# In-projection of a hybrid encoder layer: casts of the weights placed behind the copy that empties the product's bank, on ScalarE, in all blocks of tokens

## The chip, the cores and the metric

One core of a Trainium2 chip runs the whole kernel. The metric is the device time of one execution in microseconds (us). Before the change the median of three runs is 2311.37 us (2309.41 to 2311.43). The profile is of a further execution of its own, which took 2306.19 us.

## What is computed

The reference is one layer of a streaming encoder, applied to a prompt of 2048 tokens and to a batch of 8 sample sequences of 16 tokens each. Cut to what matters here:

```python
qm, km, vm, om, ip, fp, qa, ka, va = split_in(x @ w_in)        # the in-projection, D_MODEL = 1024
km = km * (M_HEAD_DIM ** -0.5)
hm, C1, n1, m1 = mlstm_chunkwise(qm, km, vm, logi, logf, C0, n0, m0, mchunk)   # 4 heads of 128
hm = (sigmoid(om) * head_norm(hm, g_mlstm_norm))
qa, ka = rope(qa, pos), rope(ka, pos)
ha = swa_prompt(qa, ka, va, attn_sinks)                        # window attention, 8 heads of 64
mix = concatenate([hm, ha], axis=-1) @ w_out                   # the out-projection
h = layer_norm(DEEPNORM_ALPHA * x + mix, ln1_g, ln1_b)
f, conv_rows = conv_ffn(h, conv_prev, w_up, w_conv, b_conv, w_down)
y = layer_norm(DEEPNORM_ALPHA * h + f, ln2_g, ln2_b)
```

The first line is the stage that the change touches. Its result is split into q and k of the mLSTM (a matrix memory with gates), its values v, its output gate, two small gates, and q, k and v of the window attention.

## The kernel before, in words

**Stages.** The kernel goes through the in-projection (about the first 620 us), the out-projection, the up-projection with its convolution (L1874) and the down-projection (L2084). TensorE does all the matrix products. Each operand in float32 is first split into a high half and a low half in a reduced format, and three products replace one (high by high, high by low, low by high). The split of one unit of weights is two instructions in `split`: a cast on ScalarE (L218) from the raw weights `wraw` to the high half, and a subtraction on VectorE (L219) that leaves the low half. VectorE's part needs the result of ScalarE's.

**The in-projection.** `i_dense` (L588) walks over four blocks `b` of four token tiles each (128 tokens a tile; block 0 has the sample tile besides). In each block it walks over five groups `g` of output columns: 0 and 1 are q and k of the mLSTM, 2 is q of the attention (which then gets its rotation, `rope`), 3 is the output gate (which goes through a tanh) and 4 is v. Two by two blocks of a product are computed with seven products instead of eight, by sums of operands (the method of Strassen and Winograd); the products are numbered `s` and come in the order 1, 7, 6, 2, 5, 3, 4 or one close to it. Each product is `i_product` (L693): 24 matmuls of 128x128 by 128x256 (L705) into one of three banks of PSUM, A, B and C, which are called `dps` in the profile. Products 1 and 2 go to A, products 6, 5 and 3 to B, 7 and 4 to C. Between the products stand "direct" items, one for each token tile, for the small gates and the keys and values of the attention.

**What empties a bank.** Behind each product `i_after` (L769) is traced, at high priority. Depending on `s` it does this:

- s = 1, only at g = 0: ScalarE copies A to B (L780), so that the following products add to the sum there.
- s = 6: ScalarE copies B to a buffer (`zev` in the profile) through the small function `copy` of L772, which scales by a constant for g < 2.
- s = 2: `i_out` (L756) copies A to a buffer on ScalarE (L764, or the tanh of L761 for g = 3) and stores it to DRAM.
- s = 5: ScalarE copies B (L772), VectorE adds C to the copy, and `i_out` stores the sum.
- s = 4: VectorE adds C to the buffer of s = 6, and `i_out` stores it. ScalarE has no copy here.
- s = 3: `i_out` copies B to a buffer (L764 or L761) and stores it, and then ScalarE copies A to B for the next group (L800).

**Weights.** Behind `i_after`, `i_dense` calls `advance` (L415). It splits as many of the next units of weights as there is room for: the ring of split weights holds four units of two halves (`w` in the profile), and each product that ends frees one unit. It also issues the loads of further raw weights on SyncE's queue, into seven slots; some units are sums that are kept in DRAM and are loaded as they are. So the cast of L218 is released by the last matmul of the product that freed its place, which is also what releases the copies of `i_after`.

**Work woven in.** The class `Chains` weaves other work into the blocks, tile by tile, as the inputs of it are there: the mLSTM tiles (`m_tile`, with the matmuls `pnum` of L1212), their norm (`m_norm`: `mr` on VectorE in L1154 to L1160, `ms` on GpSimd in L1161, the scaling `hn` on ScalarE in L1167, the transpositions `pht` of L1177 on TensorE), the window attention (`swa`: scores L1304, exponentials on ScalarE L1316, their division on ScalarE L1321, the transpositions `ppt` of L1343 on TensorE, the products `ppo` of L1349), and the sample tile's attention (L1518). VectorE also takes the sums of weights for the next stages (`txy`, L851 to L857) and the rotations (`rope`).

**Order.** TensorE's order is written out by hand: the order in which the program traces its matmuls is the order in its queue. The other engines' queues are ordered by a scheduler, which weighs priorities and its own estimate of when each instruction is ready. `tc.issue_after(ins)` is a context for that scheduler: whatever is traced inside and goes to the queue of an engine that `ins` uses is put behind `ins` in that queue. It adds no wait on a result, only an order. Before the change it was used at one place and for one kind of product:

```python
680            with self.tc.issue_after(behind) if behind and b == 0 else nullcontext():
681                self.advance()
```

`behind` is what `i_after` returned, and that was an instruction only for s = 1 at g = 0 (L780), `None` otherwise.

Of the kernel before, what the change touches and what calls it, by code (L numbers as in the profile page):

```python
# [10 lines left out]
AF = mybir.ActivationFunctionType  # L11
# [18 lines left out]
KSCALE = float(np.float32(128.0 ** -0.5))  # L30
# [175 lines left out]
class Prog:  # L206
# [381 lines left out]
    def i_dense(self):  # L588
        nc, a = self.nc, self.a
        nb = len(IBLOCKS)  # L590
        last = NG - 1

        self.next_raw()
        self.x_load(0, 2)
        for _ in range(3):
            self.next_raw()
        self.x_load(0, 4)
        self.single_raw = self.tp.tile([P, KD, P], F32, name="xsr", tag="pth", bufs=2)
        nc.sync.dma_start(self.single_raw, a["xs"])
        self.angles = {}  # L600
        self.rope_load(IBLOCKS[0][2], 2)
        self.rope_load(NPT, 1)
        self.next_split()
        self.x_steps(0, "b12")
        for _ in range(3):
            self.next_split()
        self.x_steps(0, 3)
        self.x_single(1, 2)
        self.x_load(0, 1)
        self.next_raw()  # L610
        self.x_load(0, 3)
        self.x_steps(0, 1)
        self.advance()
        self.x_steps(0, 2, "t3", 7, "t2", 6)
        self.x_single(4)
        self.x_steps(0, "t1", 5, "t4")
        self.sb, self.trans = {}, None

        passages = [{1: ["load"], 7: ["t3", 7], 6: ["t2", 6], 3: [3, "t4"], 4: ["b12", "t1"]},
                    {1: ["load"], 6: ["t3"], 7: [7, "t2"], 5: [6], 3: [3, "t4"], 4: ["b12", "t1"]}]  # L620
        sums = 0
        after = None
        for item in self.items:
            if after:

                after[0] -= 1
                if after[0] == 3:
                    self.logs_of(after[1] - 1)
                if after[0] < 0:
                    self.i_done = after[1]  # L630
                    after = None
            self.chains.hold = item[0] == "t" and item[1] > 0
            if item[0] == "t":
                _, b, ti, e = item
                if ("g", e, 3) not in self.wu:
                    self.advance()
                if b not in self.gates:
                    self.gates[b] = self.tp.tile([P, 5, 8], F32, name="gates", tag="gates", bufs=2)
                ps = self.bank([P, 512], "pg") if ti == 4 else self.ib[ti % 2 * 2]
                yield from self.i_direct(b, ti, e, ps)  # L640
                self.i_keys(b, ti, ps)
                if ti == 1:
                    if b + 1 < nb:
                        self.x_steps(b + 1, 1, 2)
                    else:
                        self.release(4)
                    after = [6, b + 1]
                elif ti == 3 and b or ti == 4:
                    self.release(4)
                    self.x_steps(b, 4)  # L650
                    if b:
                        self.x_steps(b, 5)
                self.advance()
                continue
            _, b, g, s = item
            if item not in self.wu:
                self.advance()
            yield from self.i_product(b, g, s)
            del self.wu[item]
            self.release(2)  # L660
            if self.trans and s != 4:
                self.i_transposes()
            with self.tc.high_priority():
                behind = self.i_after(b, g, s)
            if (b, g, s) == (0, 0, 7):
                self.t_setup()
            if (g, s) == (1, 6):
                self.rope_load(IBLOCKS[b][0], 2)
            if g == last and b + 1 < nb:
                if s == 7:  # L670
                    self.rope_load(IBLOCKS[b + 1][2], 2)
                for x in passages[b > 0].get(s, ()):
                    if x == "load":
                        self.spare = True
                        self.x_load(b + 1, 1, 2, 3, 4)
                    else:
                        self.x_steps(b + 1, x)
            if g == last and b + 1 == nb and s in (7, 5, 2, 3):
                self.x_pair(0, (7, 5, 2, 3).index(s))
            with self.tc.issue_after(behind) if behind and b == 0 else nullcontext():  # L680
                self.advance()

            if b >= nb // 2 and g < last:

                steps = (6, 2, 5) if g == last - 1 else (6, 5, 3)
                if s in steps:
                    self.d_sums(sums, steps.index(s))
                    sums += s == steps[2]
        self.sums = sums
        self.logs_of(nb - 1)  # L690
        self.chains.hold = False
# [64 lines left out]
    def i_out(self, b, g, i, j, src):  # L756

        nc = self.nc
        ev = src if i else self.zev()
        if g == 3:  # L760
            nc.scalar.activation(ev, src, AF.Tanh, scale=0.5)  # L761
            nc.vector.tensor_scalar_add(ev, ev, 1.0)
        elif not i:
            nc.scalar.copy(ev, src)  # L764
        if g == 2:
            self.rope(ev, IBLOCKS[b][2 * j], 2)
        self.i_store(b, g, i, j, ev)

    def i_after(self, b, g, s):  # L769
        nc, V = self.nc, self.nc.vector  # L770
        A, B, C = self.ib
        copy = lambda d, x: nc.scalar.activation(d, x, AF.Copy, scale=KSCALE) if g < 2 else nc.scalar.copy(d, x)  # L772

        def add(u):
            if g < 2:
                V.scalar_tensor_tensor(u, C, KSCALE, u, op0=ALU.mult, op1=ALU.add)
            else:
                V.tensor_add(u, C, u)
        if s == 1 and g == 0:
            return nc.scalar.copy(B, A).ins  # L780
        elif s == 6:
            self.u2 = self.zev()
            copy(self.u2, B)
        elif s == 2:
            self.i_out(b, g, 0, 0, A)
        elif s == 5:
            u4 = self.zev()
            copy(u4, B)
            add(u4)
            self.i_out(b, g, 1, 1, u4)  # L790
        elif s == 4:
            add(self.u2)
            self.i_out(b, g, 1, 0, self.u2)
            if b == 0:
                self.i_batch(g)
        elif s == 3:
            self.i_out(b, g, 0, 1, B)
            if g + 1 < NG:

                nc.scalar.copy(B, A)  # L800

    def i_batch(self, g):

# [1383 lines left out]
```

## Time and profile before

| | us |
|---|---|
| median of three runs | 2311.37 |
| lowest and highest of them | 2309.41, 2311.43 |
| profiled execution | 2306.19 |
| its span in the profile | 2304.4 |
| mean granted clock of TensorE | 0.997 |
| TensorE busy in the span | 2279.1 |

The span goes from the first to the last recorded instruction of the profiled execution; the execution's time is 1.8 us longer than it. Times in rows of a timeline are us from the span's start, then the duration; a name in brackets tells for how long the engine was idle before and what ended that. In the rows of groups, waits and timelines, the names stand as output<-inputs, and L is the line of the kernel before. PE is TensorE's matmuls, PEld its loads of weights, DVE is VectorE, ACT is ScalarE, POOL is GpSimd and SP is SyncE. "Granted clock" is the share of full speed that the chip let TensorE have, 1.00 being all of it.

### The profile page before, as it was taken

Reading aid. Unit: us, or ns where it says so; the run is one execution under the profiler, and the core shown is the slowest. Engines: PE = TensorE matmul, PEld = TensorE weight load, DVE = VectorE, ACT = ScalarE, POOL = GpSimd, SP = SyncE. Lnnn points to the kernel's source line nnn. Section 1 sums busy time; section 2 is a strip of 40 time slices with the busy share of each in tenths; the row PEclk is TensorE's granted clock in tenths of the full one; section 3 lists DMA queues with packets and bytes.
Section 4 is the critical chain, followed back from the end, with each engine's and each line's share of the span. In section 5 each row is a group of like instructions: output and inputs, shape, how many; then the busy total and the mean of one; then the engine's idle time right before and its main releaser. Section 6 shows DMA issues by size and latency. Waiting matters only on the chain.

```text
span 2304.4 us, 39746 instructions
## 1 busy us (share of the span) xinstructions
PE 2279.1 (99%) x14293; PEld 2093.5 (91%) x14293; DVE 1807.5 (78%) x3075; ACT 1272.6 (55%) x2377; POOL 272.7 (12%) x509
## 2 busy tenths in 40 slices
PE   8999999999999999999999999999999999999998
PEld 8999999999877778999999999999999988888876
DVE  8787587787688878998778777678766786895987
ACT  4453476776766656555656555555555544444442
POOL 0001001000011210211112100003111200100100
PEclk9999999999999999999999999999999999999999
DMA  7988999999987757888778889978998786756742
GB/s 265 320 303 298 311 321 342 312 305 345 313 285 241 239 196 278 306 320 307 277 276 279 302 307 308 320 263 290 318 293 262 230 294 214 256 167 222 254 154 84
DMA packets 300165, 632.38 MB, mean 274 GB/s; under 512 B 47868, under 2 KB 141120, under 8 KB 299968
## 3 DMA queue, kind: packets, MB, share of 16 engines
q1 hardware_dynamic: 295296, 616.14, 77.8%
q0 software_dynamic: 3520, 10.56, 1.4%
q10 hardware_dynamic: 1152, 3.15, 0.4%
q8 instruction: 113, 1.85, 0.3%
q14 instruction: 84, 0.69, 0.1%
HBM read 458.11 MB, written 171.64 MB: 273 GB/s over the span
## 4 chain that ended last, share of the span: by engine, by line
PE 81%; DVE 4%; DMA 1%; issue 1%; ACT 1%; POOL 0%; SPq 0%; DVEq 0%; ACTq 0%; POOLq 0%
PE dps L1874 19%; PE fup L1874 19%; PE dps L705 7%; PE fup L2084 7%; PE dps L2084 6%; PE fht L2084 6%; PE dps L223 3%; PE dps L224 2%; PE dps L225 2%; PE ppo L1349 1%; PE psc L1304 1%; PE ppt L1343 1%; PE dps L731 1%; PE fht L1698 1%; DVE w L219 1%
## 5 line engine op out<-in xcount | busy, mean ns | idle before, releaser
L1874 PE MATMUL dps<-hh,uw 128*128 128x384 f32 (+1 forms) x1848 | 478.0, 328 | 2.1 <-DVE u L1905 2.1
L1874 PE MATMUL fup<-hh,uw 128*128 128x384 f32 (+1 forms) x1848 | 478.0, 328 | 0.0
L1874 PEld LDWEIGHTS dps<-hh,uw 128*128 128x128 f32 x1848 | 330.0, 188 | 2.4 <-DVE u L1905 2.4
L1874 PEld LDWEIGHTS fup<-hh,uw 128*128 128x128 f32 x1848 | 330.0, 188 | 0.0
L1931 DVE SCALAR_TENSOR_TENSOR cc<-u,cw,cc 128x768 f32<-128x768 f32 (+1 forms) x264 | 257.9, 977 | 63.7 <-ACT cc L1929 56.9
L1874 PE MATMUL fup<-hl,uw 128*128 128x384 f32 (+1 forms) x924 | 302.7, 328 | 0.9 <-DVE hl L219 0.9
L1874 PE MATMUL dps<-hl,uw 128*128 128x384 f32 (+1 forms) x924 | 302.3, 327 | 0.0
L705 PE MATMUL dps<-w,oh 128*128 128x256 f32 x1344 | 254.2, 284 | 0.0
L218 ACT CAST uw<-wraw 128x1024 fp32r<-128x1024 f32 x126 | 123.2, 978 | 231.4 <-PE dps L2084 122.4
L219 DVE TENSOR_TENSOR w<-wraw,w 128x1024 fp32r<-128x1024 f32 (+2 forms) x167 | 189.3, 1140 | 67.0 <-ACT w L218 64.6
L218 ACT CAST w<-wraw 128x1024 fp32r<-128x1024 f32 (+2 forms) x167 | 163.0, 984 | 121.3 <-PE dps L705 63.4
L705 PEld LDWEIGHTS dps<-w,oh 128*128 128x128 f32 x1344 | 210.4, 188 | 10.9 <-issue 8.1
L219 DVE TENSOR_TENSOR uw<-wraw,uw 128x1024 fp32r<-128x1024 f32 x126 | 142.4, 1130 | 65.7 <-ACT uw L218 64.0
L705 PE MATMUL dps<-w,ol 128*128 128x256 f32 x672 | 187.8, 279 | 0.0
L1874 PEld LDWEIGHTS fup<-hl,uw 128*128 128x128 f32 x924 | 173.5, 188 | 1.6 <-DVE hl L219 1.5
L2084 PE MATMUL fup<-uw,fu 128*128 128x512 f32 x726 | 173.7, 396 | 0.0
L1874 PEld LDWEIGHTS dps<-hl,uw 128*128 128x128 f32 x924 | 173.5, 188 | 0.0
L705 PE MATMUL dps<-oh,w 128*128 128x256 f32 x896 | 169.7, 284 | 3.6 <-DVE w L219 1.3
L2084 PE MATMUL dps<-uw,fu 128*128 128x512 f32 x660 | 165.3, 396 | 1.1 <-DVE uw L219 1.1
L2084 PEld LDWEIGHTS fup<-uw,fu 128*128 128x128 f32 x726 | 136.3, 188 | 33.1
L1929 ACT ACTIVATE cc<-u,cw 128x768 f32<-128x768 f32 (+1 forms) x132 | 132.2, 1001 | 49.2 <-DVE u L1911 23.9
L2084 PEld LDWEIGHTS dps<-uw,fu 128*128 128x128 f32 x660 | 123.8, 188 | 31.5 <-DVE uw L219 1.5
(318 smaller groups left out, 4577.9 us busy)
## 6 DMA issues: line engine op xcount, KB each, us to landing
uw<-zw SPq DMA_DIRECT2D x176, 512.0 KB, 5.0
zw<-uw SPq DMA_DIRECT2D x88, 512.0 KB, 3.5
w<-zws SPq DMA_DIRECT2D x72, 512.0 KB, 5.9
wv<-wup SPq DMA_DIRECT2D x66, 512.0 KB, 4.6
wraw<-wi SPq DMA_DIRECT2D x65, 512.0 KB, 6.1
wraw<-zt SPq DMA_DIRECT2D x60, 512.0 KB, 3.9
wraw<-wdn SPq DMA_DIRECT2D x45, 512.0 KB, 4.5
wraw<-wo SPq DMA_DIRECT2D x40, 512.0 KB, 4.7
```

Of the source, the lines that this page charges most:

```text
L218: nc.scalar.copy(hi, src)
L219: nc.vector.tensor_sub(lo, src, hi.bitcast(F32))
L223: mm(out, ah, bh, start=start, stop=False)
L224: mm(out, ah, bl, start=False, stop=False)
L225: mm(out, al, bh, start=False, stop=stop)
L705: mm(o, l, r, start=s in (1, 7) and c == k == i == 0, stop=k == 3 and i == 2, skip_group_check=True)
L731: mm(o, x, w, start=k == i == 0, stop=k == KD - 1 and i == 2, skip_group_check=True)
L1304: nc.tensor.matmul(ps[kvh][:, j, :nk], q[rs, j0 + j], k[rs, sel], start=i == 0, stop=i == 2)
L1874: mm(ps, l[:, k], r[:, k], start=s in (1, 7) and k == 0 and i == 0, stop=k == 3 and i == 2, skip_group_check=True)
L1929: S.activation(c[:, v], u[:, 2:2 + n], AF.Identity, bias=w[3], scale=w[2])
L1931: V.scalar_tensor_tensor(c[:, v], u[:, i:i + n], w[i], c[:, v], op0=ALU.mult, op1=ALU.add)
L2084: mm(ps, l[:, k, c], r[:, k], start=s in (1, 4, 7) and u == 0 and k == 0 and i == 0, stop=u == nu - 1 and k == n - 1 and i == 2, skip_grou ...
```

## The change

Two things are edited. The condition `b == 0` goes, so that the ordering context is entered in each block. And `i_after` now returns, for s = 6, 2, 5 and 3 also, the ScalarE instruction that empties the bank; `i_out` returns it to `i_after`. For s = 3 with a further group to come it is the copy from A to B that is returned (the last of the two). For s = 4, and for s = 1 at g > 0, there is still nothing to return, and the call of `advance` stands as before. No instruction is added or taken away.

```diff
@@ i_dense
-            with self.tc.issue_after(behind) if behind and b == 0 else nullcontext():
+            with self.tc.issue_after(behind) if behind else nullcontext():
                 self.advance()
@@ i_out
         ev = src if i else self.zev()
+        emptied = None
         if g == 3:
-            nc.scalar.activation(ev, src, AF.Tanh, scale=0.5)
+            emptied = nc.scalar.activation(ev, src, AF.Tanh, scale=0.5).ins
             nc.vector.tensor_scalar_add(ev, ev, 1.0)
         elif not i:
-            nc.scalar.copy(ev, src)
+            emptied = nc.scalar.copy(ev, src).ins
...
         self.i_store(b, g, i, j, ev)
+        return emptied
@@ i_after
-        copy = lambda d, x: nc.scalar.activation(d, x, AF.Copy, scale=KSCALE) if g < 2 else nc.scalar.copy(d, x)
+        copy = lambda d, x: (nc.scalar.activation(d, x, AF.Copy, scale=KSCALE) if g < 2 else nc.scalar.copy(d, x)).ins
...
         elif s == 6:
             self.u2 = self.zev()
-            copy(self.u2, B)
+            return copy(self.u2, B)
         elif s == 2:
-            self.i_out(b, g, 0, 0, A)
+            return self.i_out(b, g, 0, 0, A)
         elif s == 5:
             u4 = self.zev()
-            copy(u4, B)
+            emptied = copy(u4, B)
             add(u4)
             self.i_out(b, g, 1, 1, u4)
+            return emptied
...
         elif s == 3:
-            self.i_out(b, g, 0, 1, B)
+            emptied = self.i_out(b, g, 0, 1, B)
             if g + 1 < NG:
 
-                nc.scalar.copy(B, A)
+                emptied = nc.scalar.copy(B, A).ins
+            return emptied
```

## The prediction

> **What bounds the kernel now.** I read the totals first, then the waits of the matrix engine, then single stretches. Line numbers are those of the profile of before.
>
> ```profile
> PE 2279.1 (99%) x14293; PEld 2093.5 (91%) x14293; DVE 1807.5 (78%) x3075; ACT 1272.6 (55%) x2377; POOL 272.7 (12%) x509
> ```
> ```profile
> 0.00:46.00 46.00, 38.59 (x238) 35.12 (x239) 39.32 (x66) 24.78 (x40) 0.31 (x5) 0.89 0.73 260
> 46.00:620.00 574.00, 567.93 (x4867) 538.53 (x4868) 421.42 (x971) 347.90 (x775) 46.32 (x70) 1.00 0.93 317
> 100.00:200.00 100.00, 100.00 (x868) 99.47 (x867) 81.00 (x131) 53.05 (x76) 1.92 (x3) 1.00 0.87 304
> ```
>
> TensorE bounds it. The second fence is the table of stretches (length, then busy time of PE, weight load, VectorE, ScalarE, GpSimd, then granted clock). The in-projection, the only stage that the change touches, ends near 620 us. After its first 46 us TensorE stands still for 574.00 - 567.93 = 6.1 us in all: no reordering of ScalarE there can gain more than about that. Instructions start 100/868 us = 0.115 us apart, so a product of 24 matmuls takes 2.8 us.
>
> ```profile
> PE ppt L1518 <- POOL v L1094: 2.9, 1, 2.9
> PE dps L705 <- DVE w L219: 1.3, 2, 0.8
> PE pht L1177 <- DVE ql L219: 1.1, 1, 1.1
> PE dps L705 <- ACT mr L1154: 0.9, 1, 0.9
> PE pnum L1212 <- issue: 0.5, 1, 0.5
> ```
>
> These are the waits of TensorE (total us, times, longest). They are single events: one in the sample attention (2.9), two for weights (both before 41 us), one behind ql, one that the profile puts down to mr, one at pnum. There is no steady wait for a bank to be emptied.
>
> **What the change does in the queues.** As built, the order of TensorE and GpSimd stays as it is, instruction for instruction. ScalarE, VectorE and the SP queue are reordered up to the end of the in-projection and no further. Nothing is added or removed. In ScalarE's queue 47 of the 167 casts of weights now stand behind copies of a product's bank that they stood ahead of. The usual place before:
>
> ```profile
> 57.63 1.05 ACT L218 CAST w<-wraw 128x1024 fp32r<-128x1024 f32 x1 [1.26 <-PE dps L705]
> 58.58 0.58 ACT L834 COPY zev<-pxt 128x512 f32<-128x512 f32 x1
> 59.06 0.59 ACT L764 COPY zev<-dps 128x512 f32<-128x512 f32 x1
> 59.69 0.57 ACT L800 COPY dps<-dps 128x512 f32<-128x512 f32 x1
> ```
>
> Cast and copies are released by the end of the same product; the cast went first, so the copies came 0.95 us later (58.58 - 57.63). Now they go first and the cast starts up to 1.7 us later.
>
> *Copies earlier.* A bank is written again after at least one other product (2.8 us), and cast plus copies took 2.6 us (57.63 to 60.26), so the copy was mostly in time and moving it is worth nothing. Once it was not:
>
> ```profile
> 327.01 1.04 ACT L218 CAST w<-wraw 128x1024 fp32r<-128x1024 f32 x1
> 327.95 0.59 ACT L772 ACTIVATE zev<-dps 128x512 f32<-128x512 f32 x1
> 327.37 0.28 PE L705 MATMUL dps<-oh,w 128*128 128x256 f32 x1
> 328.60 0.38 PE L705 MATMUL dps<-oh,w 128*128 128x256 f32 x1 [0.95 <-ACT mr L1154]
> ```
>
> The matmul after 327.37 waits until the copy ends (327.95 + 0.59), whatever the name in brackets. In the new order the copy stands ahead of that cast and of four divisions. The gap goes: 1.23 between starts less 0.115 is 1.1 us.
>
> *Casts later.* They feed products that lie three or more ahead (some 8 us), and since 41 us TensorE waited for no weight. 1.7 us of delay and the VectorE half behind it (1.22 us) stay inside that: zero. The SP queue's loads of raw weights wait for the cast and go 1 or 2 us later, with the same cover; without it each late unit would cost up to 1.7 us.
>
> *VectorE's side effects.* In the first tile of block 1 the low half of a weight (L219) now stands behind the step that pnum waits for:
>
> ```profile
> 318.86 1.21 DVE L219 TENSOR_TENSOR w<-wraw,w 128x1024 fp32r<-128x1024 f32 x1
> 319.99 0.68 DVE L1133 TENSOR_TENSOR dt<-pscore,dt 128x512 f32<-128x512 f32 x1
> 320.77 0.46 PE L1212 MATMUL pnum<-v,dt 128*128 128x129 f32 x2 [0.48 <-issue]
> ```
>
> pnum starts 0.1 us after L1133 ends. L1133 would come 1.13 us earlier, but one 0.7 us step of L854 slips in ahead: most of the 0.5 us gap goes. In block 2 the order puts L853 behind the low half of q:
>
> ```profile
> 514.26 0.69 DVE L853 TENSOR_TENSOR txy<-txy 128x512 f32<-128x512 f32 x1
> 514.87 0.68 DVE L219 TENSOR_TENSOR ql<-pq,qh 128x512 fp32r<-128x512 f32 x1
> 515.61 0.66 PE L1177 MATMUL pht<-ident,hn 128*128 128x128 f32 x4 [1.14 <-DVE ql L219]
> ```
>
> ql gains 514.87 - 514.26 = 0.6 us, and so does pht. In the sample attention (the 2.9 us) VectorE's work ahead of the exponentials is only shuffled; I put it at 0, bounds -0.7 and +0.7 (one step of a rotary or of L853, as the row of L853 has it).
>
> *The loss.* In that same first tile the eighth division of the attention (L1321), the last one, now stands behind four scalings hn (L1167) and the copy L764, while the other three of its group stand ahead of them, behind two casts. Before, all were done early:
>
> ```profile
> 325.25 1.86 ACT L1321 ACTIVATE sc<-sc,asm 128x128 f32<-128x128 f32 x6
> 332.23 1.04 PE L1343 MATMUL ppt<-ident,sc 128*128 128x128 f32 x8
> 332.26 0.15 DVE L1160 TENSOR_TENSOR mr<-mr,bmv 128x4 f32<-128x4 f32 x1
> 332.56 1.37 POOL L1161 TENSOR_TENSOR ms<-mr,mhalf 128x4 f32<-128x4 f32 x1 [9.60 <-DVE mr L1160]
> 333.96 0.69 ACT L1167 ACTIVATE hn<-hn,ms 128x128 f32<-128x128 f32 x2 [2.89 <-POOL ms L1161]
> 334.56 0.57 ACT L764 COPY zev<-dps 128x512 f32<-128x512 f32 x1
> 335.07 0.74 PE L1177 MATMUL pht<-ident,hn 128*128 128x128 f32 x3
> 336.30 0.33 PE L1177 MATMUL pht<-ident,hn 128*128 128x128 f32 x1 [0.48 <-ACT hn L1167]
> ```
>
> hn waits for GpSimd's ms, which waits for VectorE's mr; TensorE's eighth transposition (332.23 + 7 x 0.11 = 333.0) needs that division. Behind the waiting hn are the copy, the division and TensorE. The new times: mr loses one L219 ahead of it (-1.2) and gains a reciprocal (+0.2), so 331.3; ms 331.6 to 332.9; four hn at 0.30 to 0.35 until 334.2; copy until 334.7; division (1.86/6 = 0.3) until 335.0. The transposition moves from 333.0 to 335.0, and TensorE, which comes there 1.1 + 0.5 us sooner, stands 2.0 + 1.6 = 3.6 us. The hn then no longer hold pht (335.07 + 3 x 0.11 = 335.4 against 336.30: 0.9 saved). Net from 318 to 337, the gains there included: +2.0 - 0.9 = +1.1. If VectorE brings mr no earlier, everything is 1.0 later: +2.1. Neither excludes the other; I take +1.5.
>
> A long hold costs more than itself, as the start shows:
>
> ```profile
> 39.45 0.39 PE L705 MATMUL dps<-oh,w 128*128 128x256 f32 x1 [0.68 <-ACT w L218]
> 40.79 0.39 PE L705 MATMUL dps<-oh,w 128*128 128x256 f32 x1 [0.84 <-DVE w L219]
> 40.00:42.00 2.00, 1.21 (x7) 1.21 (x8) 2.00 (x3) 2.00 (x3) 0.00 (x0) 0.83 0.96 379
> 42.00:44.00 2.00, 2.00 (x12) 2.00 (x11) 2.00 (x4) 0.24 (x1) 0.00 (x0) 0.50 0.58 174
> 44.00:46.00 2.00, 1.31 (x8) 1.11 (x8) 1.97 (x3) 0.79 (x2) 0.00 (x0) 0.82 0.83 215
> 250.00:255.00 5.00, 2.15 (x21) 1.87 (x19) 1.00 (x4) 1.70 (x8) 1.19 (x2) 1.00 0.95 315
> ```
>
> After two gaps of 0.7 and 0.8 us the granted clock is short by (0.17 + 0.50 + 0.18) x 2 = 1.7 us. The 2.9 us of the sample attention left it at 1.00. A hold of 3.6 us is longer than both; I count the 1.7 (bounds 0 and 1.7). [...]
>
> The sum: +1.5 + 1.7 - 0.6 = +2.6 us. The profiled execution took 2306.19 us, its span 2304.4; so 2308.8 for it. The median of the runs shown, 2311.37, lies 5.2 above that execution, hence **2314.0 us**.
>
> **The rivals.** *Only the gains (A).* If ms is early enough, nothing is held at ppt, and 1.1 + 0.5 + 0.9 + 0.6 = 3.1 us go: 2308.3. For it: copies do go first. Against: hn waited 2.89 us for GpSimd where it stands now. Its limit is 6.1 us, 2305.3.
>
> *Casts behind waiting copies delay VectorE (B), slower.* VectorE runs its queue in order too, and its low halves wait for casts already:
>
> ```profile
> DVE w L219 <- ACT w L218: 60.2, 49, 4.9
> ```
>
> With the cast 0.6 us later (one copy), what stands behind an L219 on VectorE (mr, dt, ql) is 0.6 us later; it counts where TensorE has less margin than that, as ql at 515.61 has none. [...] Eight tiles are woven into the blocks; from all eight on it is 8 x 0.6 = 4.8 us more: 2318.8. Against: VectorE is idle a quarter of the stretch (421.42 of 574).
>
> *The change does nothing (C).* If the copies were never late and the division is in time after all: 2311.4. The one copy at 327.95 speaks against.
>
> **How the numbers follow.** Forecast 0.47, A 0.17, B 0.28, C 0.08. 0.2% is 4.6 us, about what a measurement of this kernel can tell from no change. Faster by more needs A near its limit: 0.08. Slower by more than 4.6 (above 2316.0) is B, plus 0.05 for a forecast whose hold is longer than worked out: 0.33. The rest, 0.59, is within. The range goes from A's limit, 2305, to B with its own upper bounds: 2318.8 + 1.7 (a second stretch at half clock) + 0.6 (2.1 in place of 1.5) + 0.7 = 2322. The forecast alone, with 0.9 and 2.1 + 1.7 + 0.7, spans 2312 to 2316.
>
> **What would show it.** A new wait of TensorE at ppt L1343 of 3 to 4 us near 331, with hn and a copy just ahead of the division on ScalarE, and a granted clock under 1.00 in the microseconds after it: right. The gaps at pnum (320.8) and before 328.6 gone: right. No such wait at ppt: A. Many new waits of 0.3 to 1 us at pht, pnum and ppo: B. TensorE waiting for weights (L219) after 46 us would make the zero for the casts wrong, and a shift after 620 us the claim that only this stage moves.

## The result, and the profile after

Over 20 runs each the changed kernel takes 2311.47 us (2310.06 to 2315.33) and the kernel before 2308.07 us (2303.73 to 2311.43). The ratio is 1.0015, with a 95% interval of 1.0010 to 1.0021: the change costs 3.4 us (2.3 to 4.8). A second set, shared with experiments, gives 1.0019 (1.0010 to 1.0028). Two of the three runs from which the prediction started are the longest of the twenty, so its 2314.0 is 2.5 us high, though the change it forecast is 0.8 us too small.

The profiled execution after took 2315.33 us, 9.1 above the profiled one before; both lie towards the ends of their twenty. So the traces are read for places, and the sum is taken from the medians. The lines up to `i_out` keep their numbers; from there on 1 to 4 are added (L764 is now L765, L1343 is L1347), and in an experiment a few more or fewer, by its edit.

The stretch of the in-projection, from the table of stretches (the prediction shows the same row of before: PE busy 567.93, clock 1.00), and then TensorE's waits in it:

```profile
46.00:620.00 574.00, 562.62 (x4808) 534.43 (x4807) 415.22 (x962) 339.55 (x755) 47.63 (x68) 0.99 0.91 312
```
```profile
PE ppt L1347 <- ACT sc L1325: 4.4, 2, 3.9
...
PE ppt L1347 <- ACT pth L1348: 1.4, 1, 1.4
PE dps L705 <- DMA w<-zws: 1.2, 1, 1.2
PE dps L705 <- ACT dps L803: 0.9, 1, 0.9
PE ppt L1347 <- DVE C L1228: 0.7, 1, 0.7
```

TensorE now stands still for 574.00 - 562.62 = 11.4 us, against 6.1. The waits at pnum, at pht and for the copy near 328 us are no longer in the list; new on top is ppt, behind a division (L1325), which is the hold. In time order, from the timeline of after:

```profile
329.22 0.99 ACT L1325 ACTIVATE sc<-sc,asm 128x128 f32<-128x128 f32 x3 [1.12 <-DVE asm L1323]
329.68 0.95 PE L1347 MATMUL ppt<-ident,sc 128*128 128x128 f32 x5 [0.48 <-ACT sc L1325]
329.93 2.50 POOL L1165 TENSOR_TENSOR ms<-mr,mhalf 128x4 f32<-128x4 f32 x1 [9.15 <-ACT sc L1325]
332.46 1.28 ACT L1171 ACTIVATE hn<-hn,ms 128x128 f32<-128x128 f32 x4 [2.25 <-POOL ms L1165]
333.64 0.56 ACT L765 COPY zev<-dps 128x512 f32<-128x512 f32 x1
334.11 0.40 ACT L1325 ACTIVATE sc<-sc,asm 128x128 f32<-128x128 f32 x1
334.56 0.47 PE L1347 MATMUL ppt<-ident,sc 128*128 128x128 f32 x1 [3.94 <-ACT sc L1325]
```

ScalarE runs three divisions, then waits 2.25 us for GpSimd with hn at the head of its queue; the four hn, a copy and only then the eighth division follow, and TensorE's eighth transposition has waited 3.94 us for it. What that does to the clock, from the table of stretches (granted clock behind the five busy times):

```profile
332.00:334.00 2.00, 0.00 (x0) 0.00 (x0) 1.62 (x3) 1.54 (x5) 1.01 (x2) 0.75 1.06 409
334.00:336.00 2.00, 1.44 (x7) 1.44 (x8) 0.00 (x1) 2.00 (x5) 0.19 (x1) 0.50 0.84 328
336.00:338.00 2.00, 2.00 (x11) 2.00 (x11) 1.78 (x2) 2.00 (x6) 0.00 (x0) 0.50 0.56 185
338.00:340.00 2.00, 2.00 (x12) 2.00 (x11) 0.33 (x2) 0.62 (x3) 0.00 (x0) 0.55 1.01 335
```

The clock is short by (0.25 + 0.50 + 0.50 + 0.45) x 2 = 3.4 us, that is half clock for 6.8 us; of these TensorE had work in the last 5.2 (1.44 + 2.00 + 1.80). At half clock the matmuls of a product start 0.21 us apart (336.33 to 336.97 for three) in place of 0.115, so it lost about 2.5 us there. What the whole place costs is read from two matmuls that stand on either side of it, in before and in after:

```profile
320.01 0.28 PE L705 MATMUL dps<-oh,w 128*128 128x256 f32 x1
339.01 1.08 PE L1349 MATMUL ppo<-pth,kva 128*64 128x512 f32 x4
```
```profile
318.30 0.28 PE L705 MATMUL dps<-oh,w 128*128 128x256 f32 x1
342.11 1.08 PE L1353 MATMUL ppo<-pth,kva 128*64 128x512 f32 x4
```

Before, 19.00 us lie between them, after 23.81: the place costs 4.8 us net, gains and clock included.

Behind it there is more. In the last block (b = 3) VectorE stands at the first step of a sum (txy), which waits for its load; the rows are of after and of before:

```profile
544.85 0.69 DVE L855 TENSOR_TENSOR txy<-txy 128x512 f32<-128x512 f32 x1 [7.47 <-DMA txy<-wdn]
```
```profile
536.28 0.69 DVE L851 TENSOR_TENSOR txy<-txy 128x512 f32<-128x512 f32 x1 [3.71 <-DMA txy<-wdn]
```

Behind that step stand VectorE's update of C (the wait of 0.7 at ppt in the list) and mr, on which hn waits, and behind hn the copies pth (the 1.4). The load is late on the queue of SP, here of before and then of after:

```profile
524.67 0.42 SPq L857 DMA_DIRECT2D zt<-txy  x1
528.52 0.37 SPq L750 DMA_DIRECT2D zqk<-zev  x1
528.94 0.54 SPq L845 DMA_DIRECT2D txy<-wdn  x1
```
```profile
533.52 0.37 SPq L750 DMA_DIRECT2D zqk<-zev  x1
533.95 0.62 SPq L861 DMA_DIRECT2D zt<-txy  x1
538.99 0.33 SPq L849 DMA_DIRECT2D txy<-wdn  x1
```

The store of the last sum (zt) used to be ahead of the store of a product (L750), which waits for ScalarE's copy; now it is behind it, and the next load, which needs the same buffer, waits for that store to land: SP's queue stands 4.3 us at it.

### The profile page after: what moved, and what is told of

Read it like the earlier page. It is cut to its first block, busy times and chain, and to the rows that moved or that the text cites. A ratio compares the mean times of both kernels' runs of the same rounds, so it can differ in the third digit from the quotient of the medians.

```text
span 2313.6 us, 39735 instructions
## 1 busy us (share of the span) xinstructions
PE 2282.5 (99%) x14293; PEld 2097.3 (91%) x14293; DVE 1807.5 (78%) x3075; ACT 1272.1 (55%) x2377; POOL 282.7 (12%) x509
## 4 chain that ended last, share of the span: by engine, by line
PE 81%; DVE 4%; DMA 1%; issue 1%; ACT 1%; SPq 0%; POOL 0%; DVEq 0%; ACTq 0%; POOLq 0%
PE dps L1878 19%; PE fup L1878 19%; PE dps L705 8%; PE fup L2088 7%; PE dps L2088 6%; PE fht L2088 6%; PE dps L223 3%; PE dps L224 2%; PE dps L225 2%; PE ppo L1353 1%; PE ppt L1347 1%; PE psc L1308 1%; PE dps L731 1%; PE fht L1702 1%; DMA txy<-wdn 1%
## 5 line engine op out<-in xcount | busy, mean ns | idle before, releaser
L219 DVE TENSOR_TENSOR w<-wraw,w 128x1024 fp32r<-128x1024 f32 (+2 forms) x167 | 189.1, 1142 | 59.4 <-ACT w L218 54.8
L219 DVE TENSOR_TENSOR uw<-wraw,uw 128x1024 fp32r<-128x1024 f32 x126 | 142.7, 1132 | 64.3 <-ACT uw L218 64.0
```

What stands on the lines that cost most here:

```text
L219: nc.vector.tensor_sub(lo, src, hi.bitcast(F32))
```

## The experiments

Theory H: the change costs what the hold of TensorE at ppt and the clock behind it cost. Rival B: casts behind copies make VectorE, the loads and with them much else late. T (the loads of the sums) and L (TensorE runs so close to its loads that time won is given back) came up on the way. All ratios are to the kernel before, run on the same chip. The sets a1 and e1 to e3, e4 to e7, e8 and e9, and e10 and e11 ran on four chips, so medians are compared within a set and ratios across.

| run | median, us | ratio (95%) |
|---|---|---|
| a1, the change again | 2313.46 | 1.0019 (1.0010 to 1.0028) |
| e1, one product taken out | 2309.82 | 1.0003 (0.9994 to 1.0012) |
| e2, last block only | 2308.33 | 0.9998 (0.9989 to 1.0007) |
| e3, all but the last block | 2315.67 | 1.0030 (1.0021 to 1.0039) |
| e4, the change, division first | 2311.36 | 1.0011 (1.0002 to 1.0020) |
| e5, third block only | 2311.03 | 1.0005 (0.9996 to 1.0014) |
| e6, before again | 2309.54 (one run) | |
| e7, as e3, again | 2318.82 (one run) | |
| e8, before, sums later | 2311.39 | 1.0021 (1.0010 to 1.0033) |
| e9, the change, sums later | 2319.09 | 1.0053 (1.0039 to 1.0066) |
| e10, before with a hold alone | 2317.55 | 1.0032 (1.0020 to 1.0044) |
| e11, as e4, one sum later | 2313.96 | 1.0023 (1.0013 to 1.0033) |

**The change again.** No edit.

> The changed kernel as it is, a second profile of it. Theory H (the eighth division of the first attention tile stands behind hn on ScalarE and holds TensorE at ppt, and the hold spoils the clock): about 2311.5 us, a wait at ppt near 330 us of 3.5 to 4.5 us, a granted clock under 1.00 just behind it; the other new gaps of the first profile (1.1 us near 370, 1.4 near 393, 2.4 near 546 to 553) are accidents of that execution and are mostly gone. Theory B (casts behind copies make VectorE, SP's loads and with them much else late): the same time, but these other gaps come again at the same places, 4.9 us in all.

TensorE's waits in this execution:

```profile
PE ppt L1347 <- ACT sc L1325: 4.4, 2, 3.9
...
PE dps L705 <- DMA w<-zws: 0.8, 1, 0.8
...
PE ppt L1347 <- ACT pth L1348: 0.6, 1, 0.6
```

The hold comes again to the tenth. Of the other new waits, the 0.9 for the copy L803 and the 0.7 behind C are gone, and those for w and behind pth are there at 0.8 and 0.6. The wait for w is not the same one, though: it stands at 393.7 us in the first profile and at 579.6 in this one. Of the 4.9 us that B wanted at the same places, only the 0.6 behind pth comes again, so here H is nearer. Still, both profiles wait for w somewhere, and neither profile of before does behind 46 us.

**The hold taken away, by one product.**

```diff
-            with self.tc.issue_after(behind) if behind else nullcontext():
+            with self.tc.issue_after(behind) if behind and (b, g, s) != (2, 0, 5) else nullcontext():
```

> The change with one product (b = 2, g = 0, s = 5) taken out of it; as built this puts the eighth division ahead of hn again, and moves few other instructions. H: the hold of about 4 us and the clock loss of 1.5 us go, the 1.0 us gap before the product behind it and 0.7 us at pht come back: 2311.5 - 3.8 = 2307.7 us, equal to before. B: 54 of 55 places are as in the change: 2310.5 to 2312 us.

```profile
PE pht L1181 <- ACT hn L1171: 2.0, 3, 1.1
```

No hold, 2.0 us at pht in its place, and 3.6 us less than the change on the same chip (2313.46 - 2309.82), where H said 3.8. With one product taken out, nothing clear of noise is left of the loss. The same two matmuls on either side of the place, in e1:

```profile
319.61 0.28 PE L705 MATMUL dps<-oh,w 128*128 128x256 f32 x1
338.89 1.08 PE L1353 MATMUL ppo<-pth,kva 128*64 128x512 f32 x4
```

They lie 19.3 us apart: 0.3 more than before, where the change had 4.8 more (5.0 in a1).

**The hold alone, in the kernel before.** In `swa`, for t = 0, the last of the eight divisions is not issued with the others:

```diff
-            self.nc.scalar.activation(hn[:, h], hn[:, h], AF.Copy, scale=s[:, h:h + 1])
+            self.scaled = self.nc.scalar.activation(hn[:, h], hn[:, h], AF.Copy, scale=s[:, h:h + 1]).ins
...
+                if t == 0 and j == 3 and len(z) == 2 and sc is z[1][0]:
+                    self.last_division = lambda: nc.scalar.activation(sc[:, 3, :N], sc[:, 3, :N], AF.Copy, scale=sm[:, 3:4])
+                    continue
...
+                    if t == 0 and (kt, kvh, j) == (0, 1, 3):
+                        with self.tc.issue_after(self.scaled):
+                            self.last_division()
                     nc.tensor.transpose(pp[:, j * P:(j + 1) * P], scs[j // 2][...], self.ident)
```

> The kernel before with the last division of the first attention tile alone moved on ScalarE: behind hn, and with it behind two copies, a cast and the first copy of ppt; nothing of the change is in it. The division comes near 338.0 us (the last hn ends at 336.2, then 1.05 + 0.56 + 0.3), TensorE wants it at 333.0: a hold of 5.0 us, less 0.9 at pht behind it, and 1.7 us of clock. H (a hold of TensorE costs its length to the end): 2308.7 + 5.8 = 2314.5 us. Theory L (TensorE runs so close to its loads that a hold is partly given back in shorter waits later): 2310 to 2312 us. B: 2308.7 us.

The waits of TensorE:

```profile
PE ppt L1349 <- ACT sc L1322: 5.2, 1, 5.2
...
PE pht L1177 <- DVE ql L219: 2.5, 1, 2.5
```
The two matmuls around the place:

```profile
319.54 0.28 PE L705 MATMUL dps<-oh,w 128*128 128x256 f32 x1
344.28 1.08 PE L1355 MATMUL ppo<-pth,kva 128*64 128x512 f32 x4
```

A hold of 5.2 us, with nothing else of the change, costs 7.4 us by the ratio (4.6 to 10.2), which bears H out; nothing is given back here, against L. The place itself costs 5.7 us (24.7 against 19.0), where H said 5.8. What goes beyond lies elsewhere and is not shown to come from the hold: the wait at ql grew from 1.1 us (before) to 2.5, and one of 1.8 us is new near 1650 us, far behind the in-projection (see the end).

Counted in this way, the place separates the runs: it takes 23.6 to 24.0 us in the four profiles of the change's hold (after, a1, e3, e7), 19.0 and 19.1 in the two of before, and 19.0 to 19.8 in the five of the change, or of parts of it, without the hold and with the sums where they were (e1, e2, e4, e5, e11).

**By blocks.**

```diff
-            with self.tc.issue_after(behind) if behind else nullcontext():
+            with self.tc.issue_after(behind) if behind and (b == 3 or (b, g, s) == (0, 0, 1)) else nullcontext():
```

For the run of all but the last block the condition is `b != 3`, for that of the third block `b == 2`, each with the same exception.

> The change in the last block (b = 3) alone. H: no hold, only the gain at ql near 515 us (1.1 us): 2307.0 us, at or just under before. B: the load of txy that waits for the store of the sums, and with it VectorE's work and ppt near 546 to 553 us, is late by itself: + 2.4 - 1.1 = 2309.5 us.

> The change in the blocks b = 0, 1 and 2, as before in the last. H: the whole loss is there, and the gain at ql is not: 2312 us. B: the loss of the last block (1.3 us net) is gone: 2310 us.

> The change in the block b = 2 alone, the one into which the first attention tile is woven; as built all eight divisions stand ahead of hn. H: gains without the hold: 0.7 (pnum) + 1.1 (before 328.6) + 0.5 (pht): 2308.6 - 2.3 = 2306.3 us. B: a third of the loss: 2310 us.

The last block alone costs nothing (0.9998): its wait at ql is gone, and in exchange VectorE waits longer for its sum and 1.1 us are lost at ppt. So B's mechanism for the last block is there in this profile and just pays for the gain; the second profile of before (below) shows how much of such waits is chance:

```profile
537.24 0.69 DVE L855 TENSOR_TENSOR txy<-txy 128x512 f32<-128x512 f32 x1 [6.38 <-DMA txy<-wdn]
```

All but the last block holds TensorE as the change does and keeps the old order in the last one; by H it should have cost what the change costs, and it cost 7 us (0.0030 x 2308.87). The third block alone should have won 2.3 us, since it has the gains and not the hold. It won nothing (1.0005): here the expectation missed. Two of its waits:

```profile
PE ppo L1353 <- ACT pth L1348: 1.8, 1, 1.8
PE pht L1181 <- DVE ql L219: 1.7, 1, 1.7
```

pnum and the gap near 328 us are gone, but at the place itself the wait for hn has grown from 0.5 to 1.1 us and two of 0.5 us for copies are new, so it takes 19.8 us in place of 19.0; behind it a wait at ppo is new and the one at ql has grown. The parts don't add up: -0.5 for the last block and +7 for the others make more than the 3.4 to 4.4 of the whole. In e3 the place costs no more than in the change (23.6 us); 1.5 us of its 7 are a wait near 1645 us that no profile of the change has, and the gain at ql is missing.

**Second looks.** e6 is the kernel before and e7 the kernel of e3, each with another profile.

> The kernel before, a second profile of it, to tell what is its own from what an execution adds by chance. H and B alike: waits at pnum, before 328.6, at pht near 335 and at pht near 515 us again; nothing over 0.3 us at ppt or ppo between 330 and 345; VectorE's wait for the load of txy near 535 us under 4.5 us. Single stretches of 3.4 us at half clock may come or go.

> The change in the blocks b = 0, 1 and 2 once more; nine executions of it took 2311 to 2319 us while the one with a profile took 2311.5. H: if this execution is one of 2315 or more, it has a further stretch of 3.4 us at a granted clock of about 0.5 behind a wait of TensorE, 1.7 us for each, and no more waits than the first. B: it has waits of 1 us or more after 340 us that the first has not, for weights, txy or copies.

The kernel before waits at the expected places, but ppo shows 1.8 us where the first profile showed none, and VectorE waited 5.32 us for the sum's load near 537 us (3.71 in the first). So waits behind such loads of 1 to 2 us are in part chance. In e7 TensorE waits 5.5 us in such places, and it was 2318.82. Of these, 3.2 us lie in the last block; the 2.3 at ppt come at 660.9 us, behind the in-projection, and there the clock is short by 1.7 us as well (0.89 over 655 to 670 us; 1.00 in e3). So both sides of that expectation came: new waits, which B had and H had not, and a further stretch at half clock, as H said.

```profile
PE ppt L1347 <- ACT pth L1348: 2.3, 1, 2.3
PE ppo L1353 <- ACT pth L1348: 1.6, 1, 1.6
PE pht L1181 <- DVE ql L219: 1.6, 1, 1.6
```

**The hold taken away by priority.**

```diff
-        divided(*z[1])
+        with self.tc.high_priority() if t == 0 else nullcontext():
+            divided(*z[1])
```

> The whole change, with the last four divisions of the first attention tile alone at high priority, so that none of them stands behind hn on ScalarE; the copy still goes ahead of its casts there. H: no hold of 3.9 us at ppt near 330 and no clock loss behind it, and the gap before 328 us stays gone too; against the change (2312.2 us over both sets of runs) - 3.9 - 1.5 + 0.5 (hn holds pht for a moment instead) = 2307.3 us, 1 to 2 us under before. B: 2311 to 2313 us, as the change.

The hold is gone, but only about two microseconds were won, within the noise (1.0011 against 1.0019). The gap near 328 us did not stay gone: at 326.33 TensorE waits 0.79 us for the copy, which now stands behind the four divisions. The first fence has rows of the timeline (VectorE, ScalarE, TensorE, and then SP's queue), the second two rows of the table of stretches:

```profile
352.51 0.69 DVE L855 TENSOR_TENSOR txy<-txy 128x512 f32<-128x512 f32 x1 [3.63 <-DMA txy<-wdn]
...
353.37 0.51 ACT L1320 ACTIVATE sc<-sc,amx 128x257 f32<-128x257 f32 x1 [5.51 <-DVE amx L1315]
...
354.99 0.38 PE L705 MATMUL dps<-w,oh 128*128 128x256 f32 x1 [2.27 <-ACT zev L765]
345.23 2.64 SPq L456 DMA_DIRECT2D wraw<-wi  x2
349.24 0.33 SPq L850 DMA_DIRECT2D txy<-wdn  x1
```
```profile
356.00:358.00 2.00, 2.00 (x13) 2.00 (x12) 2.00 (x4) 2.00 (x7) 0.00 (x0) 0.63 1.03 287
358.00:360.00 2.00, 2.00 (x11) 2.00 (x11) 1.97 (x5) 0.97 (x3) 0.00 (x0) 0.52 0.59 213
```

With TensorE 4 us earlier, the load of the next sum, queued on SP behind two loads of weights, is the late one. VectorE stands at its first step, the maximum amx behind it, on ScalarE two exponentials wait for amx and the copy of the bank behind them, and TensorE for the copy: 2.3 us, and again 1.7 us of clock. From the end of the place (ppo) to 360 us on the clock of before the same matmuls take 25.2 us here and 21.0 in before and in each of the four profiles with the hold: one hold had covered the next.

**The sums later.** For g < 3 the load of a sum is issued behind s = 2, its steps behind VectorE's addition of s = 4.

```diff
-                steps = (6, 2, 5) if g == last - 1 else (6, 5, 3)
-                if s in steps:
-                    self.d_sums(sums, steps.index(s))
-                    sums += s == steps[2]
+                steps = (6, 2, 5) if g == last - 1 else (2, 4, 4)
+                if s == steps[0]:
+                    self.d_sums(sums, 0)
+                if s == steps[1]:
+                    with self.tc.issue_after(self.added):      # the addition of s = 4
+                        self.d_sums(sums, 1)
...
```

> The kernel before with the sums of the down-projection's weights (txy) moved: their load is issued one or two products later (behind s = 2), their four VectorE steps and the store behind the addition of s = 4, for g < 3. Theory T (VectorE stands in order at the first step of a sum while its load is late, 11 to 12 us in all in the in-projection of before, and what stands behind it is what TensorE waits for): VectorE's waits for the load fall under 3 us, the waits at pht near 515 us (0.6 to 1.1) and at ppo near 548 (0.3 to 1.8) go: 2309 - 2 = 2307 us. Against T (the waits of VectorE cost nothing): 2309 us.

> The change with the same move of the sums. As built, all eight divisions of the first attention tile now stand ahead of hn, so there is no hold either, and the copy near 328 us is ahead of its casts. H and T together (the change costs its hold, and the late sums that its order brings, and nothing else): no waits of 1 us or more after 300 us, 1 us under the run before it: 2306 us. B (casts behind copies are late by themselves, for VectorE, the ring and the loads): 2 us or more over that run, 2309 to 2311 us, with waits for weights or copies.

Both missed. TensorE now waits for the weights themselves, in the run with the change twice as long as in the one without (2.1 us):

```profile
PE dps L710 <- DMA w<-zws: 4.9, 2, 3.1
```

The move also put the stores of the sums between the loads of SP's queue, so this does not tell B from T; it does show that the loads of w have little to spare. For g = 1 of the block b = 2 alone, on top of the run with the division first, steps and store go behind s = 4:

> The change with the last four divisions of the first attention tile at high priority (as in the run of that name) and, for b = 2 and g = 1 alone, the four VectorE steps of the sum and its store behind the addition of s = 4 in place of behind s = 5 and s = 3. H and T: the wait of 2.3 us near 353 us, where VectorE stood at that sum's first step, goes, and the 1.5 us of clock behind it; 2311.4 - 3.8 = 2307.6 us, 1 under before. L: TensorE gets to its next loads 4 us sooner and waits there, for w from DRAM or at the next sum: 2310 us or more.

```profile
381.12 0.69 DVE L858 TENSOR_TENSOR txy<-txy 128x512 f32<-128x512 f32 x1 [2.32 <-DMA txy<-wdn]
...
387.23 0.39 PE L707 MATMUL dps<-w,oh 128*128 128x256 f32 x1 [2.01 <-ACT zev L776]
```

The wait near 353 is gone, and the same chain (late load, VectorE, amx, exponentials, copy) takes 2.0 us at the next sum. L was right here. No version beat the kernel before.

## Why the prediction was right, step by step

- *The hold.* Shown by e1 (take it out, 3.6 us less) and e10 (put it in, 7.4 us more), and by the place itself: 4.6 to 5.0 us more wherever the change's hold is, 5.7 with the hold alone, at most 0.8 without it. Predicted 3.6 us at ppt, with hn and a copy ahead of the division; it is 0.5 + 3.9, in just that order. The term that was too small is ms: taken at 1.37 us from before, it ran 2.50. mr came as early as worked out, so of its two cases (+1.1 and +2.1) the first held. The prediction called the place the first tile of block 1 and that near 514 us block 2; counted by the kernel's b they are b = 2 and b = 3. The tile and the times were right.
- *The clock.* Predicted 1.7, lost about 2.5: the clock was at half for 6.8 us, twice the 3.4 (1.7 us short) of the start, and that began 1.6 us before the hold ended. "2.9 us left it at 1.00" was one execution's luck, and so the contrast of 2.9 with 3.6 us does not hold; see below. That a hold of 3.6 us costs clock because it is longer was the author's estimate: no run shows a length from which on one does.
- *The gains.* pnum, the copy near 328 us and hn at pht: gone, as predicted. ql: the whole wait is gone, not 0.6 of 1.1.
- *The net.* Predicted +1.5 + 1.7 = 3.2 for the place, measured 4.8: the +1.1 of the first case, 1.1 us more of ms and 2.5 of clock make 4.7. For the kernel +2.6 against 3.4 (2.3 to 4.8).
- *Zero for the casts and SP's loads.* This failed in part. After 46 us TensorE did wait for weights (1.2 and 0.8 us), though not for a split half (L219), the sign that the prediction named, but for sums loaded from DRAM (w<-zws). The step overlooked was that SP's queue also carries the sums' loads: the store of the last sum went behind the store of a product. In e2 that costs what ql gains. The number was in part luck: the place cost 1.6 us more than forecast, ql gave 0.5 more, and the rest is waits of about 1 us that change from one execution to the next.
- *Rival B* has the right link, a VectorE that stands in order (7.47 us at the first step of a sum in after) with what TensorE needs behind it, but the wait is for a load, not for a cast, and it strikes at one or two places, not in all tiles. *Rival A*, all gains and no hold, was tried as e4, e5 and e11: pnum's gain comes in all three and the copy's only in e5, and they are lost again, in e5 in part at the place itself, in e4 and e11 at the next late load.
- *Nothing after 620 us:* the order is the same there. The profile of after loses about 1.5 us near 1838 us to a stretch at half clock (0.89 over 1835 to 1850 us); the first profile of before has no such stretch (1.00), the second has it.

## What to carry to other kernels

Moving a copy ahead of other work on an engine that runs its queue in order, as ScalarE did here, also moves what the scheduler puts behind it: look for the instruction that ends up behind one that waits for another engine (here a division behind hn, at which ScalarE stood 2.25 us for GpSimd), for that one place cost more here (4.8 us) than the whole change (3.4). Where the bottleneck engine stands still for 1% of a stage and the loads come just in time, a gap that is closed can come back at the next late load, as in both runs with the division first (2.3 and 2.0 us), so closing gaps one by one wins little; whether earlier loads would help was not tried. And take the base of a forecast from many runs: the median of the three shown here was 3.3 us high.

## What the runs showed of the hardware

*GpSimd's ms takes 1.03 to 2.50 us.* The same 128x4 operation took 2.50 us at this place in both profiles of the change, and 1.37 and 1.36 there in the two of before. Two stretches of after, each with ms in it (VectorE's busy time is the third, GpSimd's the fifth):

```profile
406.60:407.70 1.10, 1.10 (x11) 0.99 (x10) 1.10 (x3) 0.00 (x0) 1.02 (x1) 1.00 1.07 366
329.90:332.40 2.50, 0.72 (x5) 0.43 (x4) 2.43 (x4) 0.31 (x2) 2.47 (x2) 1.00 1.08 344
```

VectorE is busy all through both. In the long one it runs a low half of a weight and steps of a sum, in the short one ql and two short rotary steps. Steps of a sum also ran beside the 1.37 us of before, and no run tried ms beside one of these alone, so what lengthens it was not shown.

*The same gap may cost clock or not.* The sample attention's 2.9 us left the clock at 1.00 in the first profile of before; in the second the stretch reads:

```profile
250.00:260.00 10.00, 7.48 (x65) 6.50 (x65) 1.90 (x4) 3.37 (x8) 1.19 (x2) 0.83 0.74 250
```

That is 1.7 us short, which is one part of why runs of one kernel differ by 8 us. Of the fourteen profiles nine have a granted clock of 1.00 there (245 to 262 us), four are short by 1.7 us and one by 3.4. Near 1835 us TensorE waits 2.0 to 2.1 us in all fourteen; behind it seven are short by 1.7 us and seven are not. And a longer hold need not cost more: the 3.9 us of the change took 3.4 us of clock in each of its four profiles, the 5.2 us of e10 only 1.8 (0.91 over 330 to 350 us).

*Open:* near 1645 us, where the queues are those of before, TensorE waits 1.1 to 1.9 us at fup in e3, e5, e7, e9, e10 and e11, but in neither of two profiles of before and of the change. The row is of e10, the hold alone:

```profile
PE fup L1880 <- ACT ua L1901: 1.8, 1, 1.8
```

Why was not found; it is part of those runs' times.
